# A convolution without its shift, a layer norm in two passes, and two merge gates ahead of the first attention head

## The chip, the cores and the metric

The kernel runs on one core of one Trainium2 chip. The metric is the device time of one execution in microseconds, the median of the runs. A core has five engines with a queue each, worked off in order: PE (TensorE, matmuls and transposes; PEld is its weight load), DVE (VectorE), ACT (ScalarE), POOL (GpSimd) and SP (SyncE, which here issues most DMA transfers).

## The reference

One layer of a hybrid encoder block over 1024 positions of 1024 channels, float32. One projection feeds two branches and their gates; the convolution branch is the one that the change rewrites.

```python
h = rms_norm(x, g_pre)
glu_in, gate_a, q, k, v, gate_b, merge = split(h @ w_in)
# conv branch
a, b = split(glu_in)
u = a * sigmoid(b)
u = causal depthwise conv(u, 31 taps) + conv_b
mu, var = mean(u), mean((u - mu)**2)            # over the 1024 channels
y_a = (silu((u - mu) * rsqrt(var + EPS) * ln_g + ln_b) * silu(gate_a)) @ w_conv_proj
# attention branch: 8 heads, two softmax maps each, their weighted difference,
# block-causal mask, rotary on a quarter, per-head RMS norm, times silu(gate_b)
y_b = diff_attention(q, k, v, gate_b, ...) @ w_attn_proj
y = sigmoid(m_a) * y_a + sigmoid(m_b) * y_b
out = x + rms_norm(y @ w_out, g_post)
```

## The kernel before

Tiles have channels on the 128 partitions and positions along the free dimension, so a channel block is 128 x 1024. Matmuls are exact to float32 by splitting each operand into a high and a low part and adding three products. The time goes through four parts.

**Start.** `x` is normalised and transposed into the right-hand sides `B11` to `B22` and their sums `T1` to `T4`: the projection is done two output blocks at a time by Strassen's scheme with seven products instead of eight.

**Projection, `PLAN`.** The plan lists 32 pairs of blocks. A pair has seven products of 12 matmuls (L240), whose left-hand factors `wf` are made from the weights by ACT (the high part, L180) and POOL (sums, L202, and the low part, L181), in a ring of seven buffers; the weights come through SP in `wraw`, three buffers. The products land in PSUM, in a ring of six banks (`ps_g`), and DVE combines them (L525). What a pair is for stands in its letter: `u` the gated input of the convolution, `g` and `s` the two gates, `q` queries and keys, `v` values, `m` a merge gate. Gates, `qkst`, `qkH`, `th` and most other small tiles share one ring of six SBUF buffers (`small`, 128 x 512).

After each of the eight `u` pairs stands `conv(i)`, with high priority: 31 taps on DVE (L445 or L448, and L451), each adding to the accumulator `cacc` in PSUM. Then ACT copies the two halves to `cv` tiles from the ring of six (L464), POOL adds them to `S1` (L465), ACT squares them (L468), POOL adds the squares to `S2` (L470), and SP stores them. The first convolution also makes a shift: its mean over its 128 channels, which PE computes with a matmul by ones (L459). The shift is subtracted from all blocks, so that the mean of squares less the square of the mean stays accurate.

The layer norm has the tokens `l0` to `l2`: the statistics (L479), and then the blocks again, in halves of 512 positions, read, less the mean, times the root, Silu, times the gate, stored as `z` (L501 to L507).

**Attention and fillers.** Eight heads, each with scores (L840, L841), softmax on ACT and DVE, transposes and the product with the values (L882). Each head's operands come in `load_head`: two stacks `kst`, `qh`, `ql` of 0.5 MB each and the values. Between a head's steps stand pieces of a generator, `filling`: the second merge gates (`merge_gate`, L708), the splitting of `z`, the output projection of the convolution (`conv_out`, L666), and half of that of the attention (`attn_out`). `take(n)` puts in `n` pieces, eight to a merge gate, and `pieces(h, i)` says how many at each step.

**End.** The rest of the attention's projection, the merge, the output projection (L999 to L1001) and the last norm.

A scheduler orders the instructions of each engine from a simulated timeline and from the order of the program. The queues are then fixed: an instruction that waits holds up everything behind it on its engine.

Of the kernel before, what the change touches and what calls it, by code (L numbers as in the profile page):

```python
# [67 lines left out]
def block_kernel(ctx, tc, x, positions, vecs, conv_w, lambdas, g_subln, g_post,  # L68
# [370 lines left out]
    def conv(i):  # L439
        u = conved[i]  # L440
        acc = ps.tile(blk, F32, name="cacc", tag="cv", bufs=1)
        bias = vec[:, 1, i:i + 1]
        if i == 0:
            ln["S1"], ln["S2"], ln["shift"] = [wide(n, n, 1) for n in ("S1", "S2", "shift")]
            nc.vector.tensor_scalar(out=acc, in0=u[:, 0:T], scalar1=cw[:, i, 0:1], scalar2=bias,  # L445
                                    op0=ALU.mult, op1=ALU.add)
        else:
            nc.vector.scalar_tensor_tensor(out=acc, in0=u[:, 0:T], scalar=cw[:, i, 0:1], in1=ln["shift"],  # L448
                                           op0=ALU.mult, op1=ALU.subtract)
        for k in range(1, TAPS):  # L450
            nc.vector.scalar_tensor_tensor(out=acc, in0=u[:, k:k + T], scalar=cw[:, i, k:k + 1], in1=acc,  # L451
                                           op0=ALU.mult, op1=ALU.add)
        for hh in range(2):
            sl = halves[hh]
            c = small("cv")
            if i == 0:
                nc.scalar.copy(out=c, in_=acc[:, sl])
                pm = psum_g()
                nc.tensor.matmul(pm, ones_d, c, start=True, stop=True)  # L459
                nc.scalar.mul(out=ln["shift"][:, sl], in_=pm, mul=float(D // P))  # L460
                nc.vector.scalar_tensor_tensor(out=c, in0=pm, scalar=-float(D // P), in1=c, op0=ALU.mult, op1=ALU.add)
                nc.gpsimd.tensor_copy(out=ln["S1"][:, sl], in_=c)
            else:
                nc.scalar.activation(out=c, in_=acc[:, sl], func=AF.Identity, bias=bias)  # L464
                nc.gpsimd.tensor_tensor(out=ln["S1"][:, sl], in0=ln["S1"][:, sl], in1=c, op=ALU.add)  # L465
            nc.sync.dma_start(out=cv_dram[i][:, sl], in_=c)
            sq = small("csq") if i else ln["S2"][:, sl]
            nc.scalar.activation(out=sq, in_=c, func=AF.Square)  # L468
            if i:
                nc.gpsimd.tensor_tensor(out=ln["S2"][:, sl], in0=ln["S2"][:, sl], in1=sq, op=ALU.add)  # L470


    def ln_stats():

# [1 line left out]
        for n, name in enumerate(("S1", "S2")):
            for a in range(8):
                c = 16 * n + 2 * a
                nc.tensor.matmul(pm[:, c:c + 2], ln[name][:, a * P:(a + 1) * P], ones_d[:, 0:2], start=True, stop=True)  # L479
        const_cols = small("cols")  # L480
        lnr = tmp_pool.tile([P, 8], F32, name="lr", bufs=1)
        mean, var, r = [const_cols[:, 8 * n:8 * n + 8] for n in range(2)] + [lnr]
        nc.vector.tensor_copy(out=mean, in_=pm[:, 0:16:2])
        nc.vector.tensor_tensor(out=mean, in0=mean, in1=mean, op=ALU.mult)
        nc.vector.scalar_tensor_tensor(out=var, in0=pm[:, 16:32:2], scalar=EPS, in1=mean, op0=ALU.add, op1=ALU.subtract)
        rsqrt_small(var, r)
        ln["r"] = r

    def ln_half(hh):
        sl = halves[hh]  # L490
        both = ps.tile(blk, F32, name="mean_rs", tag="cv", bufs=1)
        mean, rs = both[:, :HALF], both[:, HALF:]
        nc.tensor.matmul(mean, ones_d, ln["S1"][:, sl], start=True, stop=True)
        for a in range(4):
# [4 lines left out]
        for i in range(8):
            c, g = small("cvz"), small("gaz")  # L500
            nc.sync.dma_start(out=c, in_=cv_dram[i][:, sl])  # L501
            nc.sync.dma_start(out=g, in_=ga_dram[i][:, sl])
            nc.vector.tensor_tensor(out=c, in0=c, in1=mean, op=ALU.subtract)
            nc.vector.tensor_tensor(out=c, in0=c, in1=rs, op=ALU.mult)
            nc.scalar.activation(out=c, in_=c, func=AF.Silu, scale=vec[:, 2, i:i + 1], bias=vec[:, 3, i:i + 1])
            nc.vector.scalar_tensor_tensor(out=c, in0=c, scalar=0.5, in1=g, op0=ALU.mult, op1=ALU.mult)
            nc.sync.dma_start(out=z_dram[i][:, sl], in_=c)  # L507

    def ln_part(n):
        if n == 0:  # L510
            ln_stats()
        else:
            ln_half(n - 1)
# [564 lines left out]
```

## Time and profile before

| | |
|---|---|
| median of 2 runs | 1509.11 us (1508.09 to 1510.13) |
| the profiled execution | 1508.62 us, span 1506.9 us |
| mean granted PE clock | 0.918 |
| PE, DVE, POOL, ACT busy | 1224.9, 997.2, 743.1, 545.0 us |
| taps of the convolution (DVE) | 85.5 to 670 us |
| end of the last projection (PE) | 879.5 us |
| first score matmul | 897.7 us |

The busy time of PE is modelled and includes time at half clock, in which a matmul takes twice as long. A row of a group gives an engine's busy time and the mean of one instruction, and behind the second bar the idle time of the engine just before them with what ended it. A wait is put down to the semaphore that came last. The clock is 1 or 0.5 at any time; a mean between is a mixture.

### The profile page before, as it was taken

What the parts mean: (1) busy time and instruction counts of PE and PEld (TensorE: products, weight loads), DVE (VectorE), ACT (ScalarE), POOL (GpSimd) and SP (SyncE); (2) the same over time, 40 slices, a digit from 0 to 9 for tenths busy, and PEclk for the clock granted to TensorE, in tenths of its full rate; (3) what the DMA queues carried; (4) which work ended last, traced back from release to release, by engine and by line L of the source; (5) the groups of instructions that cost most, each with busy time, mean ns of one, the idle gap of its engine ahead of it and who ended that gap; (6) DMA issues with size and microseconds to landing.
All of it is one profiled execution on the core that took longest, in us unless ns stands there. A gap on an engine that the chain in (4) does not pass through costs nothing.

```text
span 1506.9 us, 17093 instructions
## 1 busy us (share of the span) xinstructions
PE 1224.9 (81%) x5720; PEld 1008.5 (67%) x5720; DVE 997.2 (66%) x1547; ACT 545.0 (36%) x1077; POOL 743.1 (49%) x602
## 2 busy tenths in 40 slices
PE   3716989578695959849999858999689997979898
PEld 3514867466574848637787647888578885857686
DVE  4886786949495979882218717555876669833743
ACT  7512234132323332423334316444543445413321
POOL 4843776668686867754665512122522126356000
PEclk9867999889797979979999988999799999999999
DMA  5111134142424231314436678466686575567532
GB/s 203 56 42 54 59 114 138 56 168 70 154 72 154 70 125 56 126 64 146 168 110 205 212 223 231 138 172 180 173 230 200 157 214 174 166 191 248 190 112 84
DMA packets 94456, 214.83 MB, mean 143 GB/s; under 512 B 11568, under 2 KB 12032, under 8 KB 94368
## 3 DMA queue, kind: packets, MB, share of 16 engines
q1 hardware_dynamic: 91328, 204.02, 42.6%
q0 software_dynamic: 2320, 7.49, 1.6%
q10 hardware_dynamic: 720, 2.23, 0.4%
q8 instruction: 45, 0.74, 0.2%
q14 instruction: 43, 0.35, 0.1%
HBM read 145.50 MB, written 68.19 MB: 142 GB/s over the span
## 4 chain that ended last, share of the span: by engine, by line
PE 33%; DVE 8%; DMA 7%; issue 2%; ACT 1%; POOL 1%; SPq 1%; DVEq 0%; ACTq 0%; POOLq 0%
PE ps_g L240 7%; PE ps_g L666 7%; PE ps_g L708 5%; PE ps_r L882 3%; PE ps_s L840 2%; PE ps_s L841 2%; PE ps_o L999 2%; PE ps_o L1001 2%; PE ps_o L1000 2%; DMA cvz<-cv 1%; PE ps_r L869 1%; PE ps_o L666 1%; DMA kst<-qkl 1%; DVE e L862 1%; DVE nm L850 1%
## 5 line engine op out<-in xcount | busy, mean ns | idle before, releaser
L240 PE MATMUL ps_g<-B,wf 128*128 128x512 f32 x1152 | 296.1, 411 | 105.3 <-ACT qkst L411 81.5
L240 PE MATMUL ps_g<-T,wf 128*128 128x512 f32 x1536 | 365.1, 392 | 7.7 <-DVE u L525 5.8
L240 PEld LDWEIGHTS ps_g<-T,wf 128*128 128x128 f32 x1536 | 289.7, 189 | 71.3 <-DVE u L525 6.7
L240 PEld LDWEIGHTS ps_g<-B,wf 128*128 128x128 f32 x1152 | 227.7, 200 | 159.4 <-ACT qkst L411 83.2
L451 DVE SCALAR_TENSOR_TENSOR cacc<-u,cw,cacc 128x1024 f32<-128x1024 f32 x240 | 309.0, 1288 | 6.5
L181 POOL TENSOR_TENSOR wf<-wraw,wf 128x512 fp32r<-128x512 f32 x128 | 172.6, 1351 | 87.4 <-ACT wf L180 87.1
L644 POOL TENSOR_TENSOR wL<-wraw,wH 128x512 fp32r<-128x512 f32 x48 | 64.5, 1359 | 189.9 <-ACT wH L643 168.3
L181 POOL TENSOR_TENSOR wf<-wsum,wf 128x512 fp32r<-128x512 f32 x96 | 130.4, 1358 | 39.7 <-ACT wf L180 39.5
L180 ACT CAST wf<-wraw 128x512 fp32r<-128x512 f32 x128 | 79.1, 621 | 179.3 <-PE ps_g L240 172.8
L525 DVE SCALAR_TENSOR_TENSOR u<-ps_g,u 128x512 f32<-128x512 f32 x96 | 65.8, 687 | 117.2 <-PE ps_g L240 88.2
L853 ACT ACTIVATE e<-ps_s,nm 128x256 f32<-128x256 f32 (+7 forms) x128 | 95.0, 745 | 88.4 <-DVE nm L850 28.2
L180 ACT CAST wf<-wsum 128x512 fp32r<-128x512 f32 x96 | 59.4, 619 | 150.2 <-PE ps_g L240 118.7
L708 PE MATMUL ps_g<-B,wH 128*128 128x512 f32 x256 | 83.0, 403 | 10.0 <-DMA kst<-qkh 10.0
L840 PE MATMUL ps_s<-kst,qh 128*128 128x384 f32 (+4 forms) x192 | 72.0, 382 | 12.3 <-ACT e L853 8.4
L841 PE MATMUL ps_s<-kst,ql 128*128 128x384 f32 (+4 forms) x192 | 68.2, 362 | 1.6 <-DMA ql<-qkl 1.6
L862 DVE SCALAR_TENSOR_TENSOR e<-e,rz 128x128 f32<-128x128 f32 (+3 forms) x64 | 66.0, 1031 | 1.1
L850 DVE TENSOR_REDUCE nm<-ps_s 128x1 f32<-128x640 f32 (+3 forms) x64 | 65.2, 1018 | 0.8
L872 DVE TENSOR_TENSOR wtL<-ps_r,wtH 128x512 fp32r<-128x512 f32 (+2 forms) x96 | 52.0, 549 | 18.6 <-ACT wtH L871 18.5
L202 POOL TENSOR_TENSOR wsum<-wraw 128x512 f32<-128x512 f32 x32 | 43.3, 1354 | 39.5 <-DMA wraw<-w_in 37.3
L708 PEld LDWEIGHTS ps_g<-B,wH 128*128 128x128 f32 x256 | 48.6, 193 | 20.1 <-ACT wH L643 10.4
L871 ACT CAST wtH<-ps_r 128x512 fp32r<-128x512 f32 (+2 forms) x96 | 44.1, 480 | 30.4 <-PE ps_r L869 29.7
L666 PE MATMUL ps_g<-zH,wH 128*128 128x512 f32 x128 | 52.0, 406 | 3.5 <-ACT zH L643 2.8
(234 smaller groups left out, 2348.5 us busy)
## 6 DMA issues: line engine op xcount, KB each, us to landing
wraw<-w_in SPq DMA_DIRECT2D x67, 512.0 KB, 3.5
qkh<-qkH SPq DMA_DIRECT2D x32, 256.0 KB, 2.0
qkl<-qkL SPq DMA_DIRECT2D x32, 256.0 KB, 2.1
qh<-qkh SPq DMA_DIRECT2D x32, 256.0 KB, 6.8
ql<-qkl SPq DMA_DIRECT2D x32, 256.0 KB, 8.5
tbr<-tb SPq DMA_DIRECT2D x32, 256.0 KB, 3.4
cv<-cv SPq DMA_DIRECT2D x16, 256.0 KB, 2.0
sg<-th SPq DMA_DIRECT2D x16, 256.0 KB, 2.1
```

The lines of the kernel that those rows point to most:

```text
L180: nc.scalar.copy(out=f[:, 0, :], in_=src)
L181: nc.gpsimd.tensor_tensor(out=f[:, 1, :], in0=src, in1=f.bitcast(F32)[:, 0, :], op=ALU.subtract)
L240: nc.tensor.matmul(acc, f[:, l, sl], b[:, r, :], start=(start and d + n == 0), stop=False, skip_group_check=True)
L451: nc.vector.scalar_tensor_tensor(out=acc, in0=u[:, k:k + T], scalar=cw[:, i, k:k + 1], in1=acc, op0=ALU.mult, op1=ALU.add)
L525: nc.vector.scalar_tensor_tensor(out=out, in0=acc, scalar=pos if s is None else s, in1=u, op0=ALU.mult, op1=ALU.add)
L666: nc.tensor.matmul(acc, w[l][:, sl], rhs[r][d][:, halves[hh]], start=(d - first + n == 0), stop=(d == last and n == 2))
L708: nc.tensor.matmul(acc, w[l][:, sl], f[:, r, :], start=(d + n == 0), stop=(d == 7 and n == 2))
L840: nc.tensor.matmul(sv[:, a, :], qh[:, qs], k[:, ks], start=True, stop=False)
L841: nc.tensor.matmul(sv[:, a, :], ql[:, qs], k[:, ks], start=False, stop=True)
L850: nc.vector.tensor_reduce(out=nm[:, m:m + 1], in_=sv, op=ALU.max, axis=AX.XY, negate=True)
L853: nc.scalar.activation(out=e[:, :n].rearrange("p (a b) -> p a b", a=c), in_=sv, func=AF.Exp, bias=nm[:, m:m + 1], accum_out=Z[:, i, m:m + 1])
L862: nc.vector.scalar_tensor_tensor(out=es[0][:, :n], in0=es[1][:, :n], scalar=rz[:, 1:2], in1=es[0][:, :n], op0=ALU.mult, op1=ALU.add)
```

## The change

- `conv` has no shift. Every block starts with a product and the bias (`tensor_scalar`), the last tap writes the whole block to an SBUF tile `cv` (one buffer of 128 x 1024), one transfer stores it, and POOL adds it to `tot`. ACT and PE have no part in it, no squares are made, and it takes no buffers from the ring of six.
- The layer norm has two passes over whole blocks, in the buffers of `u` (two) and `cv` (one), which the convolution has left. `ln_squares` (`l0`) computes the mean, reads each block, subtracts, stores the centred block in a new array `cc`, squares on ACT, adds on POOL. `ln_roots` (`l1`) has the statistics. `ln_out` (`l2`) reads `cc` and does the rest.
- The plan has `l1` after `m2` and `l2` after `g3`, where both stood ahead of `g2`.
- The ring `wf` has eight buffers.
- The program has two merge gates (`take(4)`, the reload of `B12`, `take(4)`, `load_head(0)`, `take(8)`) ahead of the first head instead of one, with `load_head(0)` after `B12`. `pieces` is shifted to match, and `load_og(4)` and `load_og(5)` stand after head 6.

```diff
-        "m0 m1 l0 l1 g2 l2 m2 g3 m3")
+        "m0 m1 l0 g2 m2 l1 g3 l2 m3")
...
-        f = proj.tile([P, 2, HALF], F32R, name="wf", tag="wf", bufs=7)
+        f = proj.tile([P, 2, HALF], F32R, name="wf", tag="wf", bufs=8)
...
     def conv(i):
         u = conved[i]
         acc = ps.tile(blk, F32, name="cacc", tag="cv", bufs=1)
-        bias = vec[:, 1, i:i + 1]
+        a = wide("cv", "cv", 1)
+        nc.vector.tensor_scalar(out=acc, in0=u[:, 0:T], scalar1=cw[:, i, 0:1], scalar2=vec[:, 1, i:i + 1],
+                                op0=ALU.mult, op1=ALU.add)
+        for k in range(1, TAPS):
+            nc.vector.scalar_tensor_tensor(out=a if k == TAPS - 1 else acc, in0=u[:, k:k + T],
+                                           scalar=cw[:, i, k:k + 1], in1=acc, op0=ALU.mult, op1=ALU.add)
+        nc.sync.dma_start(out=cv_dram[i], in_=a)
         if i == 0:
-            ln["S1"], ln["S2"], ln["shift"] = [wide(n, n, 1) for n in ("S1", "S2", "shift")]
...
+            ln["tot"] = wide("tot", "tot", 1)
+            nc.gpsimd.tensor_copy(out=ln["tot"], in_=a)
         else:
-            nc.vector.scalar_tensor_tensor(out=acc, in0=u[:, 0:T], scalar=cw[:, i, 0:1], in1=ln["shift"],
-                                           op0=ALU.mult, op1=ALU.subtract)
...
+            nc.gpsimd.tensor_tensor(out=ln["tot"], in0=ln["tot"], in1=a, op=ALU.add)
+
+    def ln_tile(i, name):
+        if i % 3 == 2:
+            return wide(name, "cv", 1)
+        return work.tile([P, PAD + T], F32, name=name, tag="u", bufs=2)[:, 0:T]
+
+    def ln_squares():
+        mu = ps.tile(blk, F32, name="mu", tag="cv", bufs=1)
+        for sl in halves:
+            nc.tensor.matmul(mu[:, sl], ones_d, ln["tot"][:, sl], start=True, stop=True)
+        for i in range(8):
+            c = ln_tile(i, "cvr")
+            nc.sync.dma_start(out=c, in_=cv_dram[i])
+            nc.vector.tensor_tensor(out=c, in0=c, in1=mu, op=ALU.subtract)
+            nc.sync.dma_start(out=cc_dram[i], in_=c)
+            for sl in halves:
+                sq = small("csq") if i else ln["tot"][:, sl]
+                nc.scalar.activation(out=sq, in_=c[:, sl], func=AF.Square)
+                if i:
+                    nc.gpsimd.tensor_tensor(out=ln["tot"][:, sl], in0=ln["tot"][:, sl], in1=sq, op=ALU.add)
...
+    def ln_out():
+        rs = ps.tile(blk, F32, name="rs", tag="cv", bufs=1)
+        for a in range(8):
+            dg = small("diag")[:, 0:P]
...
+            nc.tensor.matmul(rs[:, a * P:(a + 1) * P], ones_d, dg, start=True, stop=True)
         for i in range(8):
...
+            c = ln_tile(i, "cvz")
+            nc.sync.dma_start(out=c, in_=cc_dram[i])
             nc.vector.tensor_tensor(out=c, in0=c, in1=rs, op=ALU.mult)
             nc.scalar.activation(out=c, in_=c, func=AF.Silu, scale=vec[:, 2, i:i + 1], bias=vec[:, 3, i:i + 1])
+            for sl in halves:
+                g = small("gaz")
+                nc.sync.dma_start(out=g, in_=ga_dram[i][:, sl])
+                nc.vector.scalar_tensor_tensor(out=c[:, sl], in0=c[:, sl], scalar=0.5, in1=g, op0=ALU.mult, op1=ALU.mult)
+            nc.sync.dma_start(out=z_dram[i], in_=c)
...
         if h == 3:
-            return (1, 1) if i >= 2 else (0, 0)
+            return 1, int(i >= 4)
         if h == 6:
-            return (1, 1) if i < 2 or i >= 5 else (0, 0)
-        return (1, 1) if h in (0, 2) else (2, 1)
+            return (0, 0) if i == 2 else (1, 1)
+        return (1, 1) if h < 3 else (2, 1)
...
     take(4)
-    nxt = load_head(0)
     for d in range(4):
...
     take(4)
+    nxt = load_head(0)
+    take(8)
     for h in range(8):
         nxt = head(h, nxt)
+        if h == 6:
+            load_og(4)
+            load_og(5)
```

The lines move by one to four, so L240 is L241 in the changed kernel, L525 is L521 and L451 is L447. The change moves instructions on all engines; three places show it.

DVE at the first convolution, before. The rows of `u_487` belong to the next pair, `g0`:

```order
L381 SCALAR_TENSOR_TENSOR u<-th,u_423 128x512
L445 TENSOR_SCALAR cacc<-u,cw,vec 128x1024
L451 SCALAR_TENSOR_TENSOR cacc<-u,cw,cacc 128x1024 x30
L461 SCALAR_TENSOR_TENSOR cv<-ps_g,cv 128x512 x2
L525 SCALAR_TENSOR_TENSOR u_487<-ps_g,u_487 128x512
```

And now, where `u_495` belongs to `g0`:

```order
L382 SCALAR_TENSOR_TENSOR u<-th,u_431 128x512
L444 TENSOR_SCALAR cacc<-u,cw,vec 128x1024
L521 SCALAR_TENSOR_TENSOR u_495<-ps_g,u_495 128x512
L447 SCALAR_TENSOR_TENSOR cacc<-u,cw,cacc 128x1024 x2
L521 SCALAR_TENSOR_TENSOR u_874<-ps_g,u_495 128x512
L447 SCALAR_TENSOR_TENSOR cacc<-u,cw,cacc 128x1024
L521 SCALAR_TENSOR_TENSOR c_892<-ps_g,u_874 128x512
```

All thirty taps stood ahead of the next pair's combinations; now the pair's combinations stand among the taps. On PE the two matmuls of the shift (L459), which stood between the products of `u0` and those of `g0`, are gone.

DVE further on, before, in the second convolution:

```order
L525 SCALAR_TENSOR_TENSOR u_1825<-ps_g,col,u_1825 128x512
L451 SCALAR_TENSOR_TENSOR cacc<-u,cw,cacc 128x1024 x3
L525 SCALAR_TENSOR_TENSOR u_1997<-ps_g,u_1997 128x512
L451 SCALAR_TENSOR_TENSOR cacc<-u,cw,cacc 128x1024 x20
L525 SCALAR_TENSOR_TENSOR u_2037<-ps_g,u_1997 128x512
```

And now, at the end of a convolution, with the last tap into `cv` and the first of the next block:

```order
L521 SCALAR_TENSOR_TENSOR u_2295<-ps_g,col,u_2295 128x512
L447 SCALAR_TENSOR_TENSOR cacc<-u,cw,cacc 128x1024 x2
L404 SCALAR_TENSOR_TENSOR ropet<-ps_g,col,snt 64x512 x2
L407 SCALAR_TENSOR_TENSOR cst<-ps_g,col,cst 128x512
L447 SCALAR_TENSOR_TENSOR cv<-u,cw,cacc 128x1024
L521 SCALAR_TENSOR_TENSOR u_2467<-ps_g,u_2467 128x512
L408 TENSOR_TENSOR cst<-cst,ropet 128x512
L444 TENSOR_SCALAR cacc<-u,cw,vec 128x1024
```

Runs of 20, 16, 16, 15, 11, 8 and 6 taps without anything between stood in seven places; the longest run now is four.

SP where the projection hands over to the attention, before. `zd` is the last block of `z`, `ta` a merge gate, `sg` the first head's gate, `kst` the first stack, and `wraw<-w_in` the weights of the first merge gate in this part:

```order
L507 DMA zd_139<-cvz 128x512
L386 DMA sg_95<-th 128x512 x2
L386 DMA sg_94<-th 128x512 x2
L391 DMA ta_111<-th 128x512 x2
L391 DMA ta_110<-th 128x512 x2
L782 DMA sg<-sg_88 128x1024
L770 DMA kst<-qkh_64 64x1024
L770 DMA kst<-qkl_68 64x1024
L642 DMA wraw<-w_in 128x512 x2
```

And now, from the seventh of the eight stores of `z` on, with the same names and `vH`, `vL` for the values of a head:

```order
L506 DMA zd_146<-cvz 128x1024
L392 DMA ta_110<-th 128x512
L778 DMA sg<-sg_88 128x1024
L766 DMA kst<-qkh_64 64x1024
L766 DMA kst<-qkl_68 64x1024
L766 DMA qh<-qkh_64 64x1024 x2
L766 DMA ql<-qkl_68 64x1024 x2
L506 DMA zd_147<-cvz 128x1024
```

```order
L766 DMA kst<-qkl_68 64x1024
L766 DMA qh<-qkh_64 64x1024 x2
L766 DMA ql<-qkl_68 64x1024 x2
L776 DMA vH<-vh_73 128x1024
L776 DMA vL<-vl_81 128x1024
L638 DMA wraw<-w_in 128x512 x2
```

The stores of `z` were all ahead of the last gates; now the last two stand beside and behind the first stack, and the weights of the merge gate stand behind both stacks and the values. On PE the last `rs` matmul stands after 40 of the 84 matmuls of `m3`, the last pair.

More of the change, by code (lines that the diff above doesn't have):

```diff
@@ L84, in block_kernel @@
     sg_dram, ga_dram, ta_dram, tb_dram = rows("sg", 8), rows("ga", 8), rows("ta", 8), rows("tb", 8)
+    cc_dram = rows("cc", 8)
     b12_dram = rows("b12", 4, (P, HALF))
@@ L443, in conv @@
+        nc.sync.dma_start(out=cv_dram[i], in_=a)
         if i == 0:
-            ln["S1"], ln["S2"], ln["shift"] = [wide(n, n, 1) for n in ("S1", "S2", "shift")]
-            nc.vector.tensor_scalar(out=acc, in0=u[:, 0:T], scalar1=cw[:, i, 0:1], scalar2=bias,
-                                    op0=ALU.mult, op1=ALU.add)
-        else:
-            nc.vector.scalar_tensor_tensor(out=acc, in0=u[:, 0:T], scalar=cw[:, i, 0:1], in1=ln["shift"],
-                                           op0=ALU.mult, op1=ALU.subtract)
@@ L450, in conv @@
[L450 to L470, printed above, removed]
@@ L473, in ln_stats @@
-    def ln_stats():
-        pm = psum_g()
[L476 to L494, printed above, removed]
+            ln["tot"] = wide("tot", "tot", 1)
+            nc.gpsimd.tensor_copy(out=ln["tot"], in_=a)
+        else:
+            nc.gpsimd.tensor_tensor(out=ln["tot"], in0=ln["tot"], in1=a, op=ALU.add)
[3 more added lines that the diff above has]
+        return work.tile([P, PAD + T], F32, name=name, tag="u", bufs=2)[:, 0:T]
@@ new lines, in ln_roots @@
+    def ln_roots():
+        pm = psum_g()
+        for a in range(8):
+            nc.tensor.matmul(pm[:, 2 * a:2 * a + 2], ln["tot"][:, a * P:(a + 1) * P], ones_d[:, 0:2],
+                             start=True, stop=True)
+        var = small("var")[:, 0:8]
+        nc.vector.tensor_scalar(out=var, in0=pm[:, 0:16:2], scalar1=EPS, scalar2=None, op0=ALU.add)
+        ln["r"] = tmp_pool.tile([P, 8], F32, name="lr", bufs=1)
+        rsqrt_small(var, ln["r"])
+    def ln_out():
+        rs = ps.tile(blk, F32, name="rs", tag="cv", bufs=1)
+        for a in range(8):
@@ L495, in ln_half @@
             dg = small("diag")[:, 0:P]
-            nc.vector.tensor_scalar(out=dg, in0=ident, scalar1=ln["r"][:, 4 * hh + a:4 * hh + a + 1], scalar2=float(D),
+            nc.vector.tensor_scalar(out=dg, in0=ident, scalar1=ln["r"][:, a:a + 1], scalar2=float(D),
                                     op0=ALU.mult, op1=ALU.mult)
@@ L499, in ln_half @@
         for i in range(8):
[L500 to L503, printed above, removed]
+            c = ln_tile(i, "cvz")
+            nc.sync.dma_start(out=c, in_=cc_dram[i])
             nc.vector.tensor_tensor(out=c, in0=c, in1=rs, op=ALU.mult)
             nc.scalar.activation(out=c, in_=c, func=AF.Silu, scale=vec[:, 2, i:i + 1], bias=vec[:, 3, i:i + 1])
-            nc.vector.scalar_tensor_tensor(out=c, in0=c, scalar=0.5, in1=g, op0=ALU.mult, op1=ALU.mult)
-            nc.sync.dma_start(out=z_dram[i][:, sl], in_=c)
+            for sl in halves:
[3 more added lines that the diff above has]
+            nc.sync.dma_start(out=z_dram[i], in_=c)
     def ln_part(n):
[L510 to L513, printed above, removed]
+        (ln_squares, ln_roots, ln_out)[n]()
     USED = ("B11", "T2", "T3", "T1", "B21", "T4", "B22")
@@ L742, in filling @@
             yield from conv_out(i)
-        for i in range(6):
+        for i in range(4):
             load_og(i)
```

## The prediction

> **What bounds the kernel now.** I read the busy times and slices of the page first, then the waits, then the order of events round the longest waits, then a table of stretches.
>
> ```profile
> PE 1224.9 (81%) x5720; PEld 1008.5 (67%) x5720; DVE 997.2 (66%) x1547; ACT 545.0 (36%) x1077; POOL 743.1 (49%) x602
> PE   3716989578695959849999858999689997979898
> PEclk9867999889797979979999988999799999999999
> ```
>
> PE is the busiest engine, but its row dips again and again in the first half, and the granted clock dips with it. The view of waits names the dips:
>
> ```profile
> PE ps_g L240 <- ACT qkst L411: 81.5, 4, 25.1
> PE ps_g L459 <- ACT cv L457: 44.4, 1, 44.4
> ACT cv L464 <- DVE cacc L451: 72.5, 5, 19.1
> POOL u L379 <- DVE cacc L451: 65.8, 5, 32.8
> PE mean_rs L493 <- POOL S L465: 17.2, 1, 17.2
> ```
>
> Six waits cost PE 81.5 + 44.4 + 17.2 = 143 us, and every chain ends at the convolution's accumulator `cacc`. One of the four `qkst` waits, in the timelines of ACT, DVE and PE (start, duration, instruction, idle time before it):
>
> ```profile
> 285.06 0.62 ACT L180 CAST wf<-wraw 128x512 fp32r<-128x512 f32 x1 [2.10 <-PE ps_g L240]
> 304.78 0.69 ACT L464 ACTIVATE cv<-cacc,vec 128x512 f32<-128x512 f32 x1 [19.10 <-DVE cacc L451]
> ...
> 309.29 0.69 ACT L411 ACTIVATE qkst<-ps_g,col 128x512 f32<-128x512 f32 x1 [0.90 <-POOL S L465]
> ...
> 278.29 26.45 DVE L451 SCALAR_TENSOR_TENSOR cacc<-u,cw,cacc 128x1024 f32<-128x1024 f32 x20
> ...
> 282.09 2.88 PE L240 MATMUL ps_g<-T,wf 128*128 128x512 f32 x12
> 310.03 5.05 PE L240 MATMUL ps_g<-B,wf 128*128 128x512 f32 x12 [25.06 <-ACT qkst L411]
> ```
>
> DVE runs twenty taps without a break. ACT stands in its queue before the copy of the finished convolution, the `qkst` copy that would free a PSUM bank stands behind it, and PE stands still. The twelve matmuls after the wait take 5.05 us, against 2.88 before it, because the clock is at half. The shift of the first convolution is the same thing with PE itself in front: its matmul L459 stands in PE's queue ahead of the next pair of blocks.
>
> The table of stretches shows what the engines could do (stretch, length, busy time and count of PE, PEld, DVE, ACT, POOL; clock, DMA share, GB/s):
>
> ```profile
> 310.00:370.00 60.00, 59.82 (x252) 48.63 (x252) 43.46 (x46) 18.28 (x32) 48.43 (x38) 0.96 0.34 115
> 545.00:602.00 57.00, 57.00 (x243) 46.98 (x242) 51.53 (x50) 17.89 (x31) 41.50 (x32) 0.96 0.24 84
> 621.00:655.00 34.00, 34.00 (x155) 28.04 (x153) 32.57 (x31) 8.69 (x15) 25.08 (x20) 1.00 0.15 48
> 85.40:749.30 663.90, 496.65 (x2123) 403.91 (x2124) 485.11 (x477) 196.04 (x331) 435.85 (x341) 0.87 0.30 100
> 749.30:879.50 130.20, 124.02 (x554) 100.79 (x553) 76.71 (x113) 50.80 (x83) 73.27 (x54) 0.99 0.53 180
> 879.50:911.80 32.30, 14.09 (x43) 10.64 (x44) 4.77 (x16) 6.75 (x17) 3.78 (x3) 0.68 0.99 264
> 911.80:1506.90 595.10, 541.16 (x2807) 455.40 (x2805) 376.97 (x848) 237.16 (x553) 173.25 (x147) 0.97 0.59 177
> ```
>
> From the first tap to the end of the `v` pairs (85.4 to 749.3) no engine is busy for more than 497 of 664 us. DVE's taps lie in lumps: in one stretch DVE has room and PE runs, in the next DVE alone runs.
>
> **The sum, stretch by stretch.** The profiled execution took 1508.6 us, 1.7 more than its span of 1506.9, and lies 0.5 under the median of 1509.1. I work in the span.
>
> *0 to 85.4.* Nothing changes: 85.4.
>
> *First tap to the end of `v3`, now 663.9.* The new convolution writes its last tap to SBUF; POOL adds the block to `tot`, and ACT has no part in it. So no ACT or PE instruction stands before the end of a convolution any more, and in the new order DVE's taps come one to four at a time between the PSUM additions. The six waits and their half clock go; what is late next is the busiest engine.
>
> ```profile
> 760.03 2.88 PE L240 MATMUL ps_g<-B,wf 128*128 128x512 f32 x12
> 762.75 2.88 PE L240 MATMUL ps_g<-T,wf 128*128 128x512 f32 x12
> L451 DVE SCALAR_TENSOR_TENSOR cacc<-u,cw,cacc x240: 1273/1290/1291, 86.9 to 669.0; 128x1024 f32<-128x1024 f32 x120
> L448 DVE SCALAR_TENSOR_TENSOR cacc<-u,cw,shift x7: 1294/2201/2323, 162.7 to 623.1; 128x1024 f32<-128x1024 f32 x7
> L445 DVE TENSOR_SCALAR cacc<-u,cw,vec x1: 1348/1348/1348, 85.5 to 85.5; 128x1024 f32<-128x1024 f32 x1
> L465 POOL TENSOR_TENSOR S<-S,cv 128x512 f32<-128x512 f32 x14 | 19.5, 1395 | 12.8 <-ACT cv L464 12.8
> L470 POOL TENSOR_TENSOR S<-S,csq 128x512 f32<-128x512 f32 x14 | 19.1, 1364 | 0.0
> ```
>
> - PE: twelve matmuls every 2.72 us at full clock, 0.227 each; 2123 of them are 481 us. Transposes are shorter and a few records may be missing, so this is about right, not exact.
> - DVE: 485.1, less 7 first taps at 2.2 that become 1.35 (6 us): 479. Tap count and tap form stay.
> - POOL: 435.9, less 28 adds of `S` (38.6 us), plus eight whole-block operations at two of the 1.395 (about 21): 418.
>
> Two engines of about 480 share the stretch, coupled through six PSUM banks. The densest stretch of before, 621 to 655, shows how well that goes: DVE 32.57 of 34 us (96%) with PE never idle. I take 480 / 0.96 = 500. The floor is 481, with no coupling loss. The upper end comes from 545 to 602, the other dense stretch, with DVE at 51.53 of 57 (90%): 534.
>
> *End of `v3` to the last projection, now 130.2.* Six pairs of 84 matmuls are 114.3. The matmuls of `mu`, of the sums and of `rs` (18 small ones) are estimated at 5. The first pass puts a mean, eight loads, subtractions and stores and sixteen squares here; its 14 POOL adds cost 19 us beside POOL's 73, its subtractions about 11 on DVE, from where as many subtractions of the old second pass go. Both fit into 120 us. What can stand on the path: PE's `mu` matmul waits for POOL's last add after the last tap (about 3 us), and the sums wait for the last squares behind `wf` work on POOL. Nothing in before shows either; from nothing to the old `mean_rs` wait of 17 us, I take 8, nearer the lower end because four pairs lie between. Sum 128.
>
> *The hand-over, now 32.3.* Here the change costs time. The second pass has moved from beside `g2` and `m2` to the last pair and beyond.
>
> ```profile
> L504 DVE TENSOR_TENSOR cvz<-cvz,mean_rs x16: 674/679/687, 800.9 to 864.5; 128x512 f32<-128x512 f32 x16
> L505 ACT ACTIVATE cvz<-cvz,vec x16: 799/816/818, 803.8 to 865.2; 128x512 f32<-128x512 f32 x16
> L506 DVE SCALAR_TENSOR_TENSOR cvz<-cvz,gaz x16: 680/1219/1776, 804.9 to 866.0; 128x512 f32<-128x512 f32 x16
> wraw<-w_in SPq DMA_DIRECT2D x67, 512.0 KB, 3.5
> zd<-cvz SPq DMA_DIRECT2D x16, 256.0 KB, 3.8
> 876.58 2.88 PE L240 MATMUL ps_g<-B,wf 128*128 128x512 f32 x12
> 889.45 1.22 PE L708 MATMUL ps_g<-B,wH 128*128 128x512 f32 x2 [10.00 <-DMA kst<-qkh]
> ```
>
> Call E the end of the last projection. The new PE order has the last `rs` matmul after 40 of the last pair's 84, so 44 x 0.227 = 10 us before E. Eight blocks go through three buffers. One round is a store (3.8), a load of 512 KB (3.5), a product (2 x 0.68), a Silu (2 x 0.82) and two gate products (2 x 0.68 with POOL idle): 11.7 us. The first block is done about 4 us before E, the seventh, two rounds later, at E + 19. On SP the first stacks stand behind the store of the seventh block, and the first merge weights behind the last store, both stacks and `v`: 0.5 MB of `sg`, 3 of stacks, 0.5 of store, 1 of `v`, 0.5 of weights, together 5.5 MB. At the 264 GB/s of the old hand-over that is 21 us, plus 2 for the split of the weights: PE starts again at E + 42, where it was E + 10. The 14.1 us of PE work that before has done by 911.8 follow: E + 56 instead of E + 32.3, a loss of 24. That the program now names `load_head(0)` after `B12` and one gate doesn't help: in the new order SP still has both stacks ahead of the weights.
>
> The Trainium skill (SBUF — State Buffer, section "SBUF: two separate sides") gives the DMA side of SBUF about 436 GB/s. By it the 5.5 MB would take 13 us and the loss would be an estimated 16; the row has the engines 99% busy at 264, so the measurement decides.
>
> *From there to the end, 595.1.* The same work. One more merge gate lies ahead of the first head and eight pieces fewer in head 1; pieces of heads 3 and 6 shift. I bound it by the idle time at the start of head 3:
>
> ```profile
> 1050.00:1120.00 70.00, 52.84 (x271) 43.51 (x270) 55.00 (x116) 36.78 (x91) 35.08 (x35) 0.85 0.73 198
> ```
>
> It could save those 17 us or add as many; I take nothing, since PE's total stays and it is busy for 541 of the 595.
>
> Sum: 85.4 + 500 + 128 + 56 + 595 = 1364, and 1.7 outside the span: 1366 us.
>
> **The rivals.**
>
> *DVE binds harder.* The lumps gone, DVE's in-order queue and PE's order, both fixed beforehand, may wait for each other at each of the eight ends of a convolution, where POOL's clearing of `u` and its add stand in front of its `wf` work. For it: POOL's 65.8 us of such waits now. Against: with eight `wf` buffers PE has over a pair in hand. At 90% the stretch is 534, and the time 1400; at 85% it is 565, 1431.
>
> *The hand-over costs nothing.* If the second pass keeps up with the last pair, or the stacks get through before the stores, the loss of 24 goes: 1342. Against: three buffers and 11.7 us a round.
>
> *The waits form again.* POOL's head of queue takes the part of ACT's, and only the 44.4 us of the shift are saved with their half clock: 1366 + 81.5 + 17.2 = 1465. Against: POOL has 16% to spare, and its waits stand for PE's only when the `wf` buffers run dry.
>
> *Slower: the taps slow down.* The rows show two prices for the same operation: 1.29 us with the accumulator in PSUM, a mean near 2.0 and up to 2.32 where the second operand is `shift` in SBUF. If POOL, working without a pause beside the taps, made the rest cost 2.0, 240 taps would grow by 0.71 each, 170 us: 1536. It decides at about 200 slowed taps, where the gain is gone, and needs nearly all to reach 2%. Against: not one of 240 taps took over 1.291 us, with POOL busy for two thirds of that stretch.
>
> **How the numbers follow.** A measurement of this kernel can tell about 2%, 30 us, from no change: faster is under 1479. The forecast has 0.60, DVE binding harder 0.17, the free hand-over 0.14, the waits again 0.05, slow taps 0.02; 0.02 is for what I don't see. The first four are all faster. Low end: the floor of 481 (-19) with the free hand-over (-24) gives 1323, and I stop at 1328, as both at once is unlikely. High end: 534 (+34) and half of the 17 of the last part: 1410. That leaves out the worse part of the second rival, the third and the fourth, under 0.2.
>
> **What would show it.** Right: no idle time of PE over 10 us between 85 and 560; `v3` ending near 585; DVE busy for over 90% there; no ACT wait on `cacc`; PE idle for some 40 us after the last projection, ended by a DMA of `wraw`; 595 from the first steady head to the end. Wrong: PE waits ended by POOL `wf` or `tot` in every convolution (third rival), taps over 1.3 us (fourth), a hand-over under 20 us (second).

## The result and the profile after

The changed kernel takes 1375.09 us (median of two runs, 1370.57 to 1379.61), a ratio of 0.9112 to before, 95% interval 0.8981 to 0.9243. Four more runs, beside the first experiments, gave 1379.46 (0.9137, 0.9096 to 0.9178). The forecast was 1366, in a range of 1328 to 1410. The profiled execution took 1379.61 us, span 1377.8; I compare it stretch by stretch with the span of before, 1506.9.

The page of the changed kernel, busy times and slices:

```profile
PE 1216.3 (88%) x5700; PEld 1007.7 (73%) x5700; DVE 973.5 (71%) x1527; ACT 528.4 (38%) x1051; POOL 740.1 (54%) x594
...
PE   3799999999899999999960699988899988979997
...
PEclk9999999999999999999985799997999999989999
```

The first half of PE's row, which dipped six times, is nearly solid now. One deep dip is left, in the 21st to 23rd slice, and the clock dips with it. The table of stretches, cut where the prediction cut it (stretch, length, busy time and count of PE, PEld, DVE, ACT, POOL; clock, DMA share, GB/s):

```profile
85.40:586.20 500.80, 479.73 (x2109) 393.75 (x2107) 476.59 (x478) 173.00 (x300) 423.89 (x322) 0.99 0.40 136
586.20:711.30 125.10, 121.72 (x538) 100.47 (x536) 51.14 (x78) 49.40 (x81) 82.63 (x65) 0.97 0.50 174
711.30:761.20 49.90, 0.03 (x1) 0.03 (x1) 12.99 (x16) 9.36 (x11) 0.01 (x1) 0.53 0.93 300
761.20:783.50 22.30, 15.14 (x48) 11.19 (x49) 5.17 (x16) 6.89 (x18) 6.26 (x5) 0.68 0.88 239
783.50:1377.80 594.30, 547.43 (x2802) 461.64 (x2800) 374.04 (x847) 235.58 (x550) 170.56 (x145) 0.95 0.58 172
```

| stretch | before | forecast | after |
|---|---|---|---|
| start, to the first tap | 85.4 | 85.4 | 85.4 |
| first tap to the end of `v3` | 663.9 | 500 | 500.8 |
| to the last projection | 130.2 | 128 | 125.1 |
| hand-over, to the first steady head | 32.3 | 56 | 72.2 |
| from there to the end | 595.1 | 595 | 594.3 |

The first stretch gives 163 us and the second 5. The hand-over takes 40 back: PE stands still for 49.9 us after the last projection, where it stood for 10.0. The view of PE's waits, over the whole span, then over the first stretch:

```profile
PE ps_g L704 <- DMA wraw<-b: 49.9, 1, 49.9
```

```profile
PE ps_g L241 <- DVE c L521: 16.1, 6, 5.3
PE ps_g L427 <- ACT vst L423: 4.9, 4, 1.3
```

No wait for `qkst`, for a shift or for `S` is left; the longest in the stretch is 5.3 us. The hand-over, from the timelines of SP and PE (start, duration, instruction, idle time before it):

```profile
706.66 0.32 SPq L506 DMA_DIRECT2D zd<-cvz  x1
...
722.69 0.32 SPq L506 DMA_DIRECT2D zd<-cvz  x1
...
736.73 0.32 SPq L506 DMA_DIRECT2D zd<-cvz  x1
738.42 0.64 SPq L766 DMA_DIRECT2D kst<-qkh  x1
...
742.37 0.55 SPq L506 DMA_DIRECT2D zd<-cvz  x1
...
751.71 1.42 SPq L638 DMA_DIRECT2D wraw<-w_in  x2
```

```profile
708.40 2.88 PE L241 MATMUL ps_g<-B,wf 128*128 128x512 f32 x12
761.17 1.22 PE L704 MATMUL ps_g<-B,wH 128*128 128x512 f32 x2 [49.89 <-DMA wraw<-b]
```

The first, fourth and seventh block are stored at 706.7, 722.7 and 736.7, one round of three buffers apart. Only behind the seventh do the first stacks go out, behind the eighth the second ones, and then the merge weights that PE waits for.

### The profile page after: what moved, and what is told of

It is laid out like the page before. It is cut to its first block, busy times and chain, and to the rows that moved or that the text cites. A ratio compares the mean times of both kernels' runs of the same rounds, so it can differ in the third digit from the quotient of the medians.

```text
span 1377.8 us, 16996 instructions
## 1 busy us (share of the span) xinstructions
PE 1216.3 (88%) x5700; PEld 1007.7 (73%) x5700; DVE 973.5 (71%) x1527; ACT 528.4 (38%) x1051; POOL 740.1 (54%) x594
## 4 chain that ended last, share of the span: by engine, by line
PE 39%; DMA 10%; DVE 7%; POOL 4%; issue 3%; ACT 2%; SPq 0%; DVEq 0%; ACTq 0%; POOLq 0%
PE ps_g L241 9%; PE ps_g L662 8%; PE ps_g L704 6%; PE ps_r L878 3%; PE ps_s L836 2%; PE ps_s L837 2%; PE ps_o L1001 2%; PE ps_o L1000 2%; PE ps_o L999 2%; DVE cacc L447 2%; PE ps_r L865 2%; PE ps_o L662 1%; DMA wraw<-zd 1%; POOL tot L477 1%; DMA qh<-qkh 1%
## 5 line engine op out<-in xcount | busy, mean ns | idle before, releaser
L241 PE MATMUL ps_g<-T,wf 128*128 128x512 f32 x1536 | 363.4, 392 | 5.7 <-DVE u L521 5.6
L241 PEld LDWEIGHTS ps_g<-T,wf 128*128 128x128 f32 x1536 | 289.4, 189 | 67.5 <-DVE u L521 5.2
L241 PE MATMUL ps_g<-B,wf 128*128 128x512 f32 x1152 | 287.6, 403 | 20.9 <-DVE c L521 16.1
L447 DVE SCALAR_TENSOR_TENSOR cacc<-u,cw,cacc 128x1024 f32<-128x1024 f32 x232 | 297.4, 1282 | 2.9
L241 PEld LDWEIGHTS ps_g<-B,wf 128*128 128x128 f32 x1152 | 223.2, 195 | 71.7 <-DVE c L521 19.0
L182 POOL TENSOR_TENSOR wf<-wraw,wf 128x512 fp32r<-128x512 f32 x128 | 174.3, 1366 | 44.2 <-ACT wf L181 44.2
L704 PE MATMUL ps_g<-B,wH 128*128 128x512 f32 x256 | 82.8, 402 | 49.9 <-DMA wraw<-b 49.9
L521 DVE SCALAR_TENSOR_TENSOR u<-ps_g,u 128x512 f32<-128x512 f32 x96 | 65.5, 684 | 62.5 <-PE ps_g L241 62.4
L858 DVE SCALAR_TENSOR_TENSOR e<-e,rz 128x128 f32<-128x128 f32 (+3 forms) x64 | 62.4, 974 | 1.1
L836 PEld LDWEIGHTS ps_s<-kst,qh 128*128 128x128 f32 x192 | 38.6, 201 | 30.0 <-ACT e L849 23.4
```

The costliest lines, as they stand in the source:

```text
L182: nc.gpsimd.tensor_tensor(out=f[:, 1, :], in0=src, in1=f.bitcast(F32)[:, 0, :], op=ALU.subtract)
L241: nc.tensor.matmul(acc, f[:, l, sl], b[:, r, :], start=(start and d + n == 0), stop=False, skip_group_check=True)
L447: nc.vector.scalar_tensor_tensor(out=a if k == TAPS - 1 else acc, in0=u[:, k:k + T], scalar=cw[:, i, k:k + 1], in1=acc, op0=ALU.mult, op1= ...
L521: nc.vector.scalar_tensor_tensor(out=out, in0=acc, scalar=pos if s is None else s, in1=u, op0=ALU.mult, op1=ALU.add)
L704: nc.tensor.matmul(acc, w[l][:, sl], f[:, r, :], start=(d + n == 0), stop=(d == 7 and n == 2))
L836: nc.tensor.matmul(sv[:, a, :], qh[:, qs], k[:, ks], start=True, stop=False)
```

## The experiments

The theory: the convolution no longer waits in ACT's queue nor in the ring of six, so no lumps of taps and no PE waits form; what then limits the first stretch is DVE at 96%; and the late second pass costs the hand-over. Eleven kernels put this to the test, besides a repeat of the changed one without an edit:

> The changed kernel once more, as the yardstick for the other runs beside it: 1370 to 1380 us, PE idle for about 50 us between the last projection and the first merge gate.

The table has for each the profiled execution's times: E is the end of the last projection, then PE's wait, and from its restart to the end. The kernels ran on several chips, each beside the kernel before, so the ratios are what compares.

| kernel | ratio to before, 95% | time | end of `v3` | E | PE's wait | restart to end |
|---|---|---|---|---|---|---|
| before | | 1509 to 1513 | 748.8 | 879.5 | 10.0 | 617.4 |
| changed, again | 0.9137 (0.9096 to 0.9178) | 1379.46 | 587.2 | 710.9 | 50.4 | 611.0 |
| e1, pass two earlier | 0.9081 (0.9029 to 0.9132) | 1372.91 | 585.0 | 724.6 | 24.0 | 613.2 |
| e2, all earlier | 0.8820 (0.8787 to 0.8853) | 1332.62 | 582.7 | 705.7 | 10.0 | 612.3 |
| e3, old attention part | 0.9124 (0.9091 to 0.9157) | 1378.56 | 587.1 | 711.3 | 49.4 | 614.1 |
| e4, ring again | 0.9933 (0.9905 to 0.9961) | 1500.36 | 709.9 | 838.9 | 51.2 | 613.0 |
| e5, ACT copies, own tile | 0.9047 (0.8985 to 0.9108) | 1364.05 | 580.2 | 707.1 | 49.8 | 602.5 |
| e6, shift's place | 0.9455 (0.9390 to 0.9521) | 1425.69 | 633.3 | 762.9 | 50.0 | 614.2 |
| e7, fewer taps | 0.9135 (0.9088 to 0.9182) | 1377.43 | 590.2 | 715.6 | 50.8 | 608.0 |
| e8, e2 and e5 | 0.8819 (0.8796 to 0.8842) | 1332.38 | 581.6 | 710.5 | 10.3 | 615.2 |
| e9, e2, seven `wf` | 0.8804 (0.8781 to 0.8828) | 1329.08 | 579.7 | 701.1 | 11.6 | 613.5 |
| e10, e2, old attention part | 0.8882 (0.8856 to 0.8908) | 1342.74 | 585.2 | 708.2 | 10.4 | 622.3 |
| e11, halves, own tile | 0.9022 (0.8987 to 0.9057) | 1365.45 | 579.1 | 705.8 | 50.1 | 609.4 |

The last column moves by up to 14 us between kernels that have the same instructions there (602.5 to 616.6, the latter in the first execution of the changed kernel), so a difference of that size in it alone says little.

**What made the waits: the ring, ACT's queue, or the shift.**

e4 puts the old way out of the accumulator back, ACT copies into halves from the ring of six, and leaves all else changed:

```diff
-            nc.vector.scalar_tensor_tensor(out=a if k == TAPS - 1 else acc, in0=u[:, k:k + T],
+            nc.vector.scalar_tensor_tensor(out=acc, in0=u[:, k:k + T],
...
+        for sl in halves:
+            a = small("cv")
+            nc.scalar.copy(out=a, in_=acc[:, sl])
+            nc.sync.dma_start(out=cv_dram[i][:, sl], in_=a)
```

> The changed kernel, but the finished convolution is again copied by ACT, in halves, into tiles of the ring of six that the gates and qkst use, and POOL adds the halves. No shift. In the order the lumps of 11 to 20 taps come back. If the shared buffers made the lumps, the four qkst waits (81.5 us), the wait at the last convolution (17) and their half clock (about 10) come back: 1465 to 1485. If only the shift and the first convolution mattered, 1380.

It took 1500.36: nearly the whole gain is gone, more than either theory expected. Its waits up to the end of `v3`, and the stretch from the first tap:

```profile
ACT cv L452 <- DVE cacc L446: 83.3, 7, 19.3
...
PE ps_g L241 <- ACT qkst L412: 71.0, 4, 23.5
...
PE ps_g L241 <- DVE u L524: 31.1, 4, 14.5
...
PE mu L470 <- POOL tot L457: 17.1, 1, 17.1
```

```profile
84.20:709.90 625.70, 497.22 (x2109) 403.98 (x2108) 481.37 (x479) 184.99 (x315) 414.53 (x330) 0.89 0.32 113
```

The picture of before is back: 119 us of PE waits in these rows, and the clock's share (497 us busy for the same 2109 matmuls that take 480). One of them in the timelines of DVE, ACT and PE:

```profile
248.86 26.45 DVE L446 SCALAR_TENSOR_TENSOR cacc<-u,cw,cacc 128x1024 f32<-128x1024 f32 x20
```

```profile
275.35 1.07 ACT L452 COPY cv<-cacc 128x512 f32<-128x512 f32 x2 [19.30 <-DVE cacc L446]
...
278.08 0.69 ACT L412 ACTIVATE qkst<-ps_g,col 128x512 f32<-128x512 f32 x1 [0.62 <-DMA cv<-cv]
```

```profile
278.82 5.06 PE L241 MATMUL ps_g<-B,wf 128*128 128x512 f32 x12 [23.50 <-ACT qkst L412]
```

e5 keeps ACT's copy but gives it the convolution's own tile, `a = wide("cv", "cv", 1)`, with one store and one add:

```diff
+        for sl in halves:
+            nc.scalar.copy(out=a[:, sl], in_=acc[:, sl])
```

> As the run with the ring, but ACT copies the halves into the block's own tile cv. ACT's queue is then as in before, the ring of six is not. If the buffers made the lumps: about 1375, with at most 5 us more for ACT. If ACT's place in the chain made them (its copy stands in the queue ahead of others): about 1465.

1364.05: no wait came back. e4 and e5 differ in more than the ring, since e4 also stores and adds in halves. e11 separates that. It is e4 with the halves in the own tile, and nothing else:

```diff
+        own = wide("cv", "cv", 1)
         for sl in halves:
-            a = small("cv")
+            a = own[:, sl]
             nc.scalar.copy(out=a, in_=acc[:, sl])
```

> As e4_ring_again in everything (ACT copies the finished convolution in two halves, each half has its own store and its own add on POOL), but the halves lie in the convolution's own tile and not in the ring of six half blocks. e4 took 1500, e5 (own tile, one store, one add) 1364, the changed kernel 1379. Theory: the place in the ring made the lumps of taps and the PE waits, so 1364 to 1385 and no PE wait over 10 us ahead of the hand-over. Rival: the halving, that is twice as many ACT, POOL and SP instructions at the end of a convolution, made them: 1500.

1365.45. In the view of waits ACT still stands before the end of each convolution, but for 19 us in all, not 83, and its row of the stretch is that of the changed kernel:

```profile
ACT cv L453 <- DVE cacc L446: 19.3, 8, 4.1
```

```profile
84.00:580.00 496.00, 479.34 (x2113) 393.85 (x2112) 473.77 (x477) 181.89 (x315) 423.91 (x329) 0.99 0.40 136
```

So the place in the shared ring is what made the lumps and the waits, and not ACT's part nor the number of instructions; between e4 and e11 lie 135 us. What the ring does to the order of the queues can be seen (e4 has runs of up to twenty taps without a PSUM addition between them, the longest of e11 has four); by which step of the scheduler it does so was not tried.

e5 and e11 are some 14 us faster than the changed kernel. About 7 of it stand at the end of `v3` (580 and 579 for 587). The rest lies later and is not settled: e8, below, adds the same edit to another order of parts and gains nothing.

e6 adds two matmuls by ones into `ps_g` after the first convolution, with ACT reading them, as the shift had them, without using the result:

```diff
             nc.gpsimd.tensor_copy(out=ln["tot"], in_=a)
+            for sl in halves:
+                pm = psum_g()
+                nc.tensor.matmul(pm, ones_d, a[:, sl], start=True, stop=True)
+                nc.scalar.copy(out=small("shift"), in_=pm)
```

> The changed kernel, and after the first convolution two matmuls by ones on its block into two banks of the ring of six PSUM banks, read by ACT, as the shift had them; the result is not used. In the order the 29 taps of the first convolution stand in one piece again. If the shift cost its place in the ring of banks, PE waits about 40 us there again: 1375 + 44 + 3 of half clock, about 1420. If it cost only its own instructions: 1378.

1425.69, 46 us slower, and the wait is that of before (44.4):

```profile
PE ps_g L455 <- DVE cv L447: 43.6, 1, 43.6
```

A matmul that stands in PE's queue ahead of work that could run costs the wait for the end of 31 taps. With e4's 121 us over the changed kernel, e6's 46 make 167; the stretch had shrunk by 163.

**What sets the pace now.** e7 leaves 7 of the 31 taps of each block out, 23 to 29. The expectation below counts 8, but the edit drops 56 taps in all (232 instructions `cacc<-u,cw,cacc` become 176), 72 us and not 82.

```diff
-        for k in range(1, TAPS):
+        for k in [*range(1, TAPS - 8), TAPS - 1]:
```

> The changed kernel without 8 of the 31 taps of each block (taps 23 to 29 and one more are left out, so the convolution is not the reference's). It takes 64 x 1.28 = 82 us of DVE from the stretch of 500.8 us, in which DVE is busy for 476.6 and PE for 479.7. If DVE sets the pace, the stretch falls to PE's 481 us, and the time by about 20 to 1355. If PE sets it, nothing moves by more than 5 us.

1377.43, no difference. The stretch and PE's waits in it:

```profile
85.40:590.40 505.00, 479.67 (x2109) 392.74 (x2107) 424.60 (x424) 174.66 (x300) 418.81 (x321) 0.99 0.41 140
```

```profile
PE ps_g L241 <- DVE c L521: 19.6, 6, 5.5
PE ps_g L427 <- ACT vst L423: 5.0, 4, 1.3
```

With 56 taps of 1.28 us less, the stretch is 505 us for 501. DVE's busy time falls by 52 and not by 72, in part because two more subtractions lie in the stretch and other instructions take longer (the rotary addition L408 1.76 us for 1.26 in the mean); DVE is then busy for 84%. So DVE's throughput does not bind. PE does: 480 us of matmuls and 21 to 25 of short waits for `c` and `vst`, which do not shrink with a DVE that has room.

**The hand-over.** Two kernels change only the order of parts. e1:

```diff
-        "m0 m1 l0 g2 m2 l1 g3 l2 m3")
+        "m0 m1 l0 g2 l1 m2 l2 g3 m3")
```

> The changed kernel with the roots ahead of m2 and the second pass ahead of g3, one pair earlier each. In the order of SP the stores of z then stand ahead of the first stacks, and the first merge weights right behind the first stack. If the late second pass makes the long hand-over (the theory), PE's wait after the last projection falls from 50 us to about the 10 of before, and the time to about 1335. If the 5 MB of stacks and values make it, whatever stands ahead of them, the wait falls to about 23 (5 MB at 264 GB/s, and 2 us to split the weights) and the time to about 1350. If the pass only moves its cost beside POOL's work, PE waits earlier instead and the time stays at 1375.

e2:

```diff
-        "m0 m1 l0 g2 m2 l1 g3 l2 m3")
+        "l0 m0 m1 g2 l1 l2 m2 g3 m3")
```

> The changed kernel with the first pass named ahead of m0, the roots after g2 and the second pass straight behind them, ahead of m2. The theory of the late second pass: no better than one pair earlier, about 1335, since the wait is then at 10 us. The rival that POOL has no room beside the weight factors: PE's wait for the squares (3 us in the changed kernel) grows to 10 or more, and the time is 1345 to 1360.

e1 took 1372.91, 7 us less than the changed kernel beside it, and the two intervals overlap: of its expectations the third fits, the cost moves. The view of waits of e1, behind the end of `v3`, shows where to:

```profile
PE ps_g L704 <- DMA wraw<-w_in: 24.0, 1, 24.0
...
PE ps_g L483 <- POOL tot L477: 17.4, 1, 17.4
```

The sums (L483) now stand on PE before POOL has added the squares, whose adds alternate with the `wf` work of the next pair. E is 14 us later, and the hand-over's wait falls only to 24, as the eighth `z` block still goes out at 736 us. e2 also starts the first pass two pairs earlier, so the sums do not wait, and its second pass is through before the last projection is (SP, then PE):

```profile
700.78 0.32 SPq L506 DMA_DIRECT2D zd<-cvz  x1
...
709.42 0.83 SPq L638 DMA_DIRECT2D wraw<-w_in  x2
```

```profile
715.69 1.22 PE L704 MATMUL ps_g<-B,wH 128*128 128x512 f32 x2 [9.95 <-DMA wraw<-b]
```

The eighth store leaves at 700.8, 5 us before E (705.7), and PE's wait is the 10 us of before. 1332.62 is 47 us less than the changed kernel on the same chip. Of the 44 us between the two profiled spans, 40 lie in this wait, and E is 5 us earlier.

e8 adds e5's edit to e2:

> The order of parts of e2 (l0 m0 m1 g2 l1 l2 m2 g3 m3) and, with it, the copy of e5: ACT copies the finished accumulator into the convolution's own tile. e2 alone took 1332.6, e5 alone 15 us less than the changed kernel. Theory: the part of e5's gain that its trace shows ahead of the hand-over holds (the last v pair ends at 580 for 586, so about 6 us), the part behind it (602 for 611 to 617 from PE's restart to the end) is scatter of the last part: 1326. Rival: the two gains add up in full: 1318, with some 602 from the restart to the end. Second rival: e5's gain is all scatter: 1333.

1332.38: the same as e2, as the second rival has it.

**Two parts that were costed at nothing.** e3 undoes the attention part of the change (one merge gate, `load_head(0)` ahead of `B12`, the old `pieces`), e10 does the same on e2, and e9 puts the ring `wf` back to seven buffers on e2:

```diff
-        f = proj.tile([P, 2, HALF], F32R, name="wf", tag="wf", bufs=8)
+        f = proj.tile([P, 2, HALF], F32R, name="wf", tag="wf", bufs=7)
```

> The changed kernel with the attention part undone: load_head(0) behind the first half of a merge gate, one gate ahead of the first head, the old pieces, the old place of load_og. The prediction took this part at nothing: 1367 to 1383. The rival that the second gate covers part of the loading: its 48 matmuls of 0.227 us are 11 us, so about 1386.

> The order of parts of e2 with the attention part of before (one merge gate, no transfers of B12 ahead of the first stacks, the old split of the pieces). In the changed kernel undoing it gave nothing (1378.6 against 1379.5), but there PE waited 50 us for the end of the transfers. Theory: the gates and transfers ahead of the stacks have no work to cover where the hand-over is short either, so nothing changes: 1333, with PE restarting about 10 us after the last projection. Rival: with the wait gone the place of the merge gates counts, and the 5 us by which the time from PE's restart to the end is shorter in e2 (612) than in before (617) go: 1338 or more, with the loss between the restart and the first steady head.

> The order of parts of e2 with seven instead of eight buffers for the split weight blocks wf. Theory: PE never waits for a wf tile in the changed kernel's trace, its idle time before the v pairs end is all on the combinations c and vst, so the eighth buffer hides nothing: 1333, and no PE wait on wf. Rival, from the prediction's words that eight buffers keep PE over a pair ahead: with seven, POOL's 21 us of whole-block adds and its 8 memsets come through at the ends of the convolutions, 8 times 2 to 4 us: 1349 to 1365, with PE waits ended by POOL wf.

e3 took 1378.56, no difference. e10 took 1342.74, and its interval touches none of those of e2, e8 and e9, which have the new attention part: the part is worth about 10 us there. The rival's time fits, but the loss does not lie where it put it. The score matmuls of the changed kernel, its repeat, e3, e2 and e10 (first and last start):

```profile
L836 PE MATMUL ps_s<-kst,qh x192: 218/362/796, 768.9 to 1190.7; 128*128 128x384 f32 x48, 128*128 128x512 f32 x48, 128*128 128x320 f32 x32, 128*128 128x448 f32 x32
```

```profile
L836 PE MATMUL ps_s<-kst,qh x192: 218/362/742, 769.9 to 1185.8; 128*128 128x384 f32 x48, 128*128 128x512 f32 x48, 128*128 128x320 f32 x32, 128*128 128x448 f32 x32
```

```profile
L836 PE MATMUL ps_s<-kst,qh x192: 218/364/741, 768.5 to 1180.8; 128*128 128x384 f32 x48, 128*128 128x512 f32 x48, 128*128 128x320 f32 x32, 128*128 128x448 f32 x32
```

```profile
L836 PE MATMUL ps_s<-kst,qh x192: 218/365/774, 724.5 to 1140.8; 128*128 128x384 f32 x48, 128*128 128x512 f32 x48, 128*128 128x320 f32 x32, 128*128 128x448 f32 x32
```

```profile
L836 PE MATMUL ps_s<-kst,qh x192: 220/362/740, 727.3 to 1144.8; 128*128 128x384 f32 x48, 128*128 128x512 f32 x48, 128*128 128x320 f32 x32, 128*128 128x448 f32 x32
```

From the last start to the end of the span it is 187 and 186 us in the two executions of the changed kernel and 194 in e3, 187 in e2 and 196 in e10: the attention part leaves 7 to 9 us less work behind the last head, in both orders. Over all kernels here it is 183 to 190 us with the new part and 194 to 196 without it (before, e3, e10). Why e3 shows nothing of it in its time stays open. From the first to the last score matmul the changed kernel takes 421.8 and 415.9 us in its two executions, and e3 412.3; kernels with the new part lie between 411 and 422 there, so one execution of each cannot tell. The four times of the changed kernel beside e3 spread from 1374.02 to 1382.18, so a few us either way are not excluded.

e9 shows that the eighth `wf` buffer hides nothing in e2: PE has no wait on `wf`, and the time is the same within the intervals. e2 and e9 beat both kernels, at 0.88 of before.

## Why the prediction was right

**The convolution's waits.** Right. "No ACT or PE instruction stands before the end of a convolution any more": the six waits are gone, the longest of PE's before the end of `v3` is 5.3 us, and DVE's taps come in short groups. But the reason that it gave was that ACT has no part any more, and the new order of the taps; the ring stands only in the description of the change. e11 shows that the ring made the lumps: with ACT back and the ring out, no lump and no wait came back. For the shift the reason holds (e6).

**480 / 0.96 = 500.** The number is right (500.8), the step behind it is not. It made DVE the binding engine, at the 96% of one dense stretch of before, and "two engines of about 480 share the stretch". DVE was busy for 95%, as forecast, and yet e7 took 72 us of taps away and the stretch stayed. What binds is the term that I had put as the floor, PE's 481 (measured 479.7), and the 21 us over it are short waits, 16.1 for combinations and 4.9 for `vst`. In the stretch that the 96% came from, 621 to 655, PE had no idle time, so it held no price of sharing for PE: that 480 / 0.96 came so near is luck. (DVE's term also takes the seven first taps at their median, 2.2; their mean is 2.01, so they save 5 us and not 6.) A busy share of 95% did not tell which of two engines of the same load would give way.

**The second stretch, 128.** 125.1. Of the 8 us taken for late waits, PE's wait for the sums was 3.35 us, and it had none for `mu`.

**The hand-over, 56.** 72.2: right in kind, short by 16, and this is where the forecast's 9 us on the median (13 on the span) lie. Two terms of the sum were mis-sized.
- "11.7 us a round", which put the seventh block at E + 19. The first block was stored at E - 4.6, as forecast, the seventh at E + 25.4: rounds of 16.0 and 14.0 us (706.66, 722.69, 736.73). The work on a block was priced rightly: 4.5 us from the fourth block's product, below, to its store, for 4.4 in the sum. The store and the load before it were not: 11.6 us from the first store to that product, where the sum has 7.3. SP issued the load only at 711.50, behind two more stores and the loads of gates, and it landed 6.7 us later. From the seventh store to PE's restart it took 24.4 us, for the 23 of the sum.

```profile
718.23 1.22 DVE L500 TENSOR_TENSOR cvz<-cvz,rs 128x1024 f32<-128x1024 f32 x1 [6.23 <-DMA cvz<-cc]
```

- "The 14.1 us of PE work that before has done by 911.8 follow." That is PE's busy time in the stretch; the time it takes is 22.3 (761.2 to 783.5), because PE waits there for transfers and has a clock of 0.68. In before it is 22.35 too (889.45 to 911.8). I added a busy time where an elapsed one belonged: 8 us.

The forecast of a price for the late second pass is confirmed by e2, which takes it back: 40 us, measured as the wait alone.

The transfers: the row of the wait shows 300 GB/s at 93% busy, that of e1's wait 314 at 98%:

```profile
724.60:748.60 24.00, 0.01 (x1) 0.00 (x0) 6.92 (x9) 6.43 (x9) 0.00 (x0) 0.61 0.98 314
```

The Trainium skill (SBUF — State Buffer, section "SBUF: two separate sides") puts the DMA side of SBUF at about 436 GB/s. No full stretch here comes near it, so the row of before, 264, was the better price, if 12 to 16% too low.

**The rest, 595.** 594.3. The attention part was costed at nothing, and e3 measured nothing. That price does not hold in general: in the order of e2 the part is worth about 10 us (e10).

**The rivals.** "DVE binds harder": no, it does not bind at all. "The hand-over costs nothing": no, but e2 makes it so. "The waits form again" through POOL: no wait of PE on `wf`. "The taps slow down": none did, with POOL busy for 85% of the stretch:

```profile
L447 DVE SCALAR_TENSOR_TENSOR cacc<-u,cw,cacc x232: 1271/1280/1291, 87.4 to 572.6; 128x1024 f32<-128x1024 f32 x116
```

## What to carry to other kernels

A tile that is filled late by a long chain of work should not come from a ring that other, urgent tiles share: here two such half tiles per convolution cost 135 us while every engine had room. Find what binds by taking work away, not by the busy share. And when a step is moved behind the last compute of a stage, count what stands behind its transfers on the queue: here 40 us of a 163 us gain went there, and another order of the same parts brought them back.

## What was not expected of the hardware

The taps read one operand in SBUF and the accumulator in PSUM, and hold 1.27 to 1.29 us with POOL busy for 85% of the stretch. Instructions of DVE with both operands in SBUF do not hold their time here. In the changed kernel's timelines the same addition of the rotary step took 2.90 and 0.69 us, and 0.83 in a third place:

```profile
286.75 0.83 DVE L408 TENSOR_TENSOR cst<-cst,ropet 128x512 f32<-128x512 f32 x1
...
346.88 2.90 DVE L408 TENSOR_TENSOR cst<-cst,ropet 128x512 f32<-128x512 f32 x1
...
361.77 0.69 DVE L408 TENSOR_TENSOR cst<-cst,ropet 128x512 f32<-128x512 f32 x1
```

```profile
285.72 1.31 POOL L182 TENSOR_TENSOR wf<-wsum,wf 128x512 fp32r<-128x512 f32 x1
286.97 1.77 POOL L182 TENSOR_TENSOR wf<-wraw,wf 128x512 fp32r<-128x512 f32 x1
...
346.69 1.30 POOL L182 TENSOR_TENSOR wf<-wsum,wf 128x512 fp32r<-128x512 f32 x1
347.94 1.30 POOL L182 TENSOR_TENSOR wf<-wraw,wf 128x512 fp32r<-128x512 f32 x1
...
358.27 1.72 POOL L182 TENSOR_TENSOR wf<-wsum,wf 128x512 fp32r<-128x512 f32 x1
363.23 1.29 POOL L416 TENSOR_TENSOR qkL<-cst,qkH 128x512 fp32r<-128x512 f32 x1 [3.23 <-ACT qkH L415]
```

The long one began beside two `wf` subtractions on POOL and ended at 349.78, half a microsecond after the second; the short one fell into POOL's pause from 360.0 to 363.2. The third began inside a POOL subtraction and ended 0.55 us after it, and POOL's next subtraction took 1.77 us instead of 1.30. The Trainium skill (SBUF — State Buffer, section "SBUF: two separate sides") says that GpSimd and DVE share one pair of SBUF ports, held for a whole instruction, and that an operation of DVE with two SBUF inputs has to wait for it when GpSimd reads SBUF. The rows agree, the taps included. Ahead of the `c` that ends PE's longest wait, 5.3 us, stands such an instruction: L407 took 2.02 us beside POOL's whole-block add, and 0.68 at its shortest. How much of PE's remaining waits comes from them was not tested.
